# A two-block model on one core: modulation products shared with POOL, own PSUM banks in the mixers, and the context's norm in step with its loads

## The chip, the cores and the metric

The kernel runs on one core of a Trainium2 chip. A core has TensorE (matrix products, written PE in the profile, its weight loads PEld), VectorE (DVE), ScalarE (ACT), GpSimd (POOL) and SyncE (SP), which here issues most transfers. The metric is the device time of one execution in microseconds, in float32, from inputs in device memory to the output there; the median of several runs is given.

## The reference, cut to what matters

Two transformer-like models run one after the other on 256 tokens of width 1024. The first has two layers; the second has one layer with a context of 256 tokens of its own and ends in 32 experts.

```python
for l in range(2):                       # first block
    sh1, sc1, g1, sh2, sc2, g2 = split(silu(c) @ ada_w[l] + ada_b[l], 6)
    h = rmsnorm(x, norm_mix_w[l]) * (1 + sc1) + sh1
    x = x + g1 * mixer(h, ...)           # attention + mLSTM, gated, merged
    h = rmsnorm(x, norm_ffn_w[l]) * (1 + sc2) + sh2
    x = x + g2 * conv_ffn(h, ...)
x = rmsnorm(x, final_norm_w)
...                                      # second block
mod_c = silu(c_ctx) @ w_ada + b_ada      # modulation of the context
hc = rmsnorm(ctx, norm1) * (1 + sc1c) + sh1c
pc = hc @ w_in                           # keys, values, states of the context
...                                      # same for x; three mixers; experts
```

The modulation (the "adaptive" products) is a row vector of 1024 times a matrix of 1024 x 6144, four times in all: for both layers, for the context (a third of it) and for the second block.

## The kernel before

Activations lie transposed, as eight blocks of 128 channels by 256 tokens. A float32 product is made of three matmuls of a rounded high part and a low rest (`mm3`, `mm3n`, lines 474 to 476 and 487 to 489): weights come from memory in loads of 128 x 2048 floats (1 MB, `Stream.reach`, `load` at L442), each half of which ACT copies to `hi` (L451) and VectorE differences to `lo` (L453), three buffers of 1024 columns each. The buffers `raw` of the loads (three) are shared with the modulation matrices outside the context; in the context these have four of their own.

Modulation isn't done on TensorE. `ada` (L524 to L536) loads 128 x 2048 floats of the transposed matrix, and VectorE multiplies each half of 1024 with the broadcast row `c` and adds it up in one instruction (L533): 16 products for the context, 144 more in the background. A background generator is moved on by `tick()`, called after steps of the foreground, with a rate per tick; `ADA_PARTS` and `ADA_RATE` say which sixths of a modulation are made in which mixer or feed-forward, and how fast.

The order within each engine comes from a scheduler that plans with the program's order as priority; `in_order` ties the weight and modulation loads to the program's order on SP.

The stages: the context of the second block first (`context`, L1163), which needs the modulation of the context, the norm of `ctx` (`norm_mod`, `rstd_x`, `scaled`) and then projections from `h`: the first four column blocks at once (`proj4`: for each of eight blocks of `h` four column blocks in two banks of tag `d`), more from `proj`, `hgrn_ctx`, `na_norm`. Then rope tables, and for each of two layers a mixer (L660) and a feed-forward (L987). Beside the feed-forwards runs a recurrence on the context (`rwkv`), then comes the middle (three mixers of the second block), then the experts.

PSUM has eight banks, of tags d (2), a (3), y (2), f (1). In the mixer the latent projections use two d banks (`proj4`) and one y bank: `p2[:, :T]` for the last query block and `p2[:, T:]` for rope keys and gates (L707 to L709), then two d banks each for keys (`keys`), values (`pv`, L733) and queries.

Of the kernel before, what the change touches and what calls it, by code (L numbers as in the profile page):

```python
# [11 lines left out]
F32 = mybir.dt.float32  # L12
# [4 lines left out]
OP = mybir.AluOpType  # L17
AX = mybir.AxisListType
PSUM = bass.MemoryType.PSUM
P = 128  # L20
# [15 lines left out]
ADA_PARTS = (range(2, 6), range(6, 9), range(9, 14), range(14, 18))  # L36
ADA_RATE, RK_RATE, MID_RATES = (0.8, 0.45, 0.95, 0.6), 0.8, (0.6, 1.0, 1.0, 1.0, 0.6)
# [314 lines left out]
class Net:  # L352
# [153 lines left out]
    def proj4(self, st, h):  # L506

        ps = [self.ps("d") for _ in range(2)]
        for i, hk in enumerate(h):
            for c in range(4):  # L510
                self.mm3(ps[c // 2][:, c % 2 * T : c % 2 * T + T], st, [hk], i == 0 and c % 2 == 0, i == 7)
        return ps
# [10 lines left out]

    def ada(self, src, c, bias, mod, parts, pool=None):  # L524

        nc = self.nc
        for s in parts:
            for q in range(4 * s, 4 * s + 4):
                raw = self.load(src[q], pool, 3 if pool is None else CX_RAW)
                for r in range(2):  # L530
                    j = 2 * q + r
                    w = raw[:, r * 1024 : r * 1024 + 1024]
                    nc.vector.scalar_tensor_tensor(w, w, 0.5, c, OP.mult, OP.mult, accum_out=mod[:, j : j + 1])  # L533
                yield
            m = slice(8 * s, 8 * s + 8)
            nc.vector.tensor_tensor(mod[:, m], mod[:, m], bias[:, m], OP.add)  # L536
# [45 lines left out]
    def scaled(self, x, r, gain, shift):  # L582

        nc = self.nc
        hhi, hlo = self.pair(self.ap, 8, "h")
        for k in range(8):
# [5 lines left out]
            if k == 0:  # L592
                self.normed = a.ins
            b = nc.vector.scalar_tensor_tensor(hlo[:, k, :], t, shift[:, k : k + 1], hhi[:, k, :].bitcast(F32), OP.add, OP.subtract)  # L594
        self.normed_v = b.ins
        return self.parts((hhi, hlo), range(8))

    def norm_mod(self, x, norm, scale, shift, adds=True):

        gain = self.np.tile([P, 8], F32, tag="gain", name=self.uid("gain"))  # L600
        self.nc.vector.scalar_tensor_tensor(gain, scale, 1.0, norm, OP.add, OP.mult)
        return self.scaled(x, self.rstd_x(x, adds), gain, shift)
# [57 lines left out]
    def mixer(self, l, mp, x, mod):  # L660
# [4 lines left out]
        h = self.norm_mod(x, self.V("nmix" + s, 0, 8), mod[:, 8:16], mod[:, 0:8])  # L665
# [39 lines left out]
        p2 = self.ps("y")  # L705
        self.mm3(p2[:, :T], st, h)
        normed(ckv, 3, 2, 256)  # L707
        latent(2, p2[:, :T], self.V("qn" + s, 2))
        self.mm3(p2[:, T:], st, h)  # L709
# [15 lines left out]
        nc.vector.tensor_tensor(krm[64:128, :], p2[64:128, T:], self.cs[64:128, :], OP.mult)  # L725
        gi, gf = self.tmp(T, "gi", bufs=1, rows=8), self.tmp(T, "gf", bufs=1, rows=8)
        nc.vector.tensor_scalar(gi, p2[0:8, T:], self.V("gb" + s)[0:8], None, OP.add)
        nc.vector.tensor_scalar(gf, p2[32:40, T:], self.V("gb" + s)[32:40], None, OP.add)
# [4 lines left out]
        pv = [self.ps("d") for _ in range(2)]  # L733
# [214 lines left out]
        for j0 in (0, 4):  # L948
            pas, pbs = ([self.ps(t) for _ in range(2)] for t in "dy")
            for ps, yp in ((pas, yap), (pbs, ymp)):  # L950
                for q in range(4):
                    self.mm3(ps[q // 2][:, q % 2 * T : q % 2 * T + T], st, yp)
                    if q % 2 and ps is pbs:
# [7 lines left out]
                        self.tick()  # L961
# [120 lines left out]
    def first(self):  # L1082
        nc, x = self.nc, self.x
        with self.pool("cxm") as cxp, self.pool("cb") as self.cbp:
            with self.pool("rope") as rp:
# [5 lines left out]
                with self.phase("r", {}):  # L1091
                    self.rope_tables(rp)
# [70 lines left out]
    def context(self, cxp, rp):  # L1163
# [3 lines left out]
        with self.pool("cx") as cx, self.phase("c", {256: 6, 512: 5}):  # L1167
# [5 lines left out]
            for i, _ in enumerate(self.ada(A["ada2"], cc, self.V("adab2", 0, 48), self.mod_c, (0, 1), cx)):  # L1173
                if i == 1:
                    nc.sync.dma_start(self.vec, A["vecs"])
                    nc.sync.dma_start(xc, A["ctxT"].rearrange("p (k t) -> p k t", k=8))
                if i == 5:
                    st.reach()
            self.cb = self.silu_row(A["c_x"], nc.sync)
            h = self.norm_mod(xc, self.V("n1", 0, 8), self.mod_c[:, 8:16], self.mod_c[:, 0:8], False)  # L1180
# [7 lines left out]
            first = self.proj4(st, h)  # L1188
# [6 lines left out]
            self.hgrn_ctx(cx, h, st)  # L1195
            for _ in self.na_norm(st, h, self.V("nk"), [self.naK[:, i : i + 2, :] for i in (0, 2)], False, "a"):
                self.tick()
# [971 lines left out]
```

## Time and profile before

| | us |
|---|---|
| median of 3 runs | 1775.16 (1772.66 to 1775.33) |
| the profiled execution | 1772.79 |
| its span, first to last instruction | 1770.9 |
| TensorE busy | 1579.1 (89%) |
| VectorE busy | 1128.0 (64%) |
| ScalarE busy | 758.6 (43%) |
| POOL busy | 77.9 (4%) |

The mean granted clock of TensorE is 0.946 of full speed. The profile comes from one execution; "idle before" in a row is the time in which the engine did nothing ahead of that instruction, and the name behind it is what came last of what it waited for. Matmuls are pipelined: each has a duration longer than its distance from the next. Shares over the whole span mix stages of different kinds, so the rows below are taken from single stretches.

### The profile page before, as it was taken

The numbers are of one execution on the slowest core, as the hardware profiler recorded it, in microseconds if no ns is written. First come the engines' busy times: TensorE is split into PE (matmuls) and PEld (weight loads), VectorE is DVE, ScalarE is ACT, GpSimd is POOL, SyncE is SP. The second block draws the span as 40 slices with busy tenths as digits, with TensorE's granted clock in tenths as the row PEclk, the third lists the DMA queues.
The fourth block names the chain that finished last, engine by engine and source line by source line (L and its number), as shares of the span: only waits on it lengthen the run. The fifth ranks groups of instructions, "written<-read, shape, count | busy, mean of one in ns | idle before, by whom it ended". The sixth has DMA issues, their size and how long they took to land.

```text
span 1770.9 us, 32054 instructions
## 1 busy us (share of the span) xinstructions
PE 1579.1 (89%) x13278; PEld 1269.7 (72%) x13278; DVE 1128.0 (64%) x2167; ACT 758.6 (43%) x1256; POOL 77.9 (4%) x81
## 2 busy tenths in 40 slices
PE   3989999999998999989999999999989877776766
PEld 2988999899998899979999999878874312221211
DVE  7979878798887898879989778766662111011011
ACT  3566545664455654556454576464431100000000
POOL 0000000020010000001010101000000000000000
PEclk7999999999999999999999999998989889888888
DMA  9745675556674478565667543123369999999998
GB/s 392 312 142 191 242 281 204 209 207 221 217 250 143 169 266 319 216 237 179 239 228 289 194 171 114 67 98 134 144 249 403 419 417 416 417 416 419 419 417 340
DMA packets 76808, 460.78 MB, mean 260 GB/s; under 512 B 8563, under 2 KB 11123, under 8 KB 28147
## 3 DMA queue, kind: packets, MB, share of 16 engines
q1 hardware_dynamic: 74352, 452.45, 67.0%
q10 hardware_dynamic: 2306, 6.24, 1.0%
q8 instruction: 106, 1.74, 0.4%
q14 instruction: 44, 0.35, 0.1%
HBM read 457.61 MB, written 1.05 MB: 259 GB/s over the span
## 4 chain that ended last, share of the span: by engine, by line
PE 63%; DMA 23%; DVE 8%; ACT 4%; issue 2%; POOL 0%; SPq 0%; DVEq 0%; ACTq 0%; POOLq 0%
DMA ew<-in_wgu 11%; PE d L474 10%; PE d L476 10%; PE d L475 10%; DMA ew<-in_wdown 8%; PE y L474 4%; PE y L476 3%; PE y L475 3%; PE a L1392 3%; DVE lo L453 2%; PE d L2052 2%; DVE raw L533 2%; PE a L1981 1%; PE a L628 1%; DMA raw<-in_ws 1%
## 5 line engine op out<-in xcount | busy, mean ns | idle before, releaser
L451 ACT CAST hi<-raw 128x1024 fp32r<-128x1024 f32 x309 | 322.4, 1048 | 303.2 <-PE d L475 186.2
L453 DVE TENSOR_TENSOR lo<-raw,hi 128x1024 fp32r<-128x1024 f32 x309 | 379.1, 1233 | 90.3 <-ACT hi L451 88.5
L474 PE MATMUL d<-hhi,hi 128*128 128x256 f32 x1320 | 387.9, 295 | 29.4 <-ACT hhi L591 23.7
L475 PE MATMUL d<-hlo,hi 128*128 128x256 f32 x1320 | 381.3, 289 | 3.2 <-DVE hlo L594 1.7
L476 PE MATMUL d<-hhi,lo 128*128 128x256 f32 x1320 | 380.2, 288 | 0.2 <-DVE lo L453 0.2
L474 PEld LDWEIGHTS d<-hhi,hi 128*128 128x128 f32 x1320 | 258.4, 196 | 38.3 <-ACT hhi L591 26.3
L475 PEld LDWEIGHTS d<-hlo,hi 128*128 128x128 f32 x1320 | 259.3, 196 | 6.6 <-DVE hlo L594 2.9
L476 PEld LDWEIGHTS d<-hhi,lo 128*128 128x128 f32 x1320 | 259.0, 196 | 1.4 <-DVE lo L453 0.4
L2052 PE MATMUL d<-ew,xe 128*32 128x512 f32 x984 | 165.3, 704 | 56.5 <-DMA ew<-in_wgu 56.0
L533 DVE SCALAR_TENSOR_TENSOR raw<-raw,cb 128x1024 f32<-128x1024 f32 x160 | 193.9, 1228 | 5.4 <-DMA raw<-in_ada 5.0
L2052 PEld LDWEIGHTS d<-ew,xe 128*32 128x32 f32 x984 | 26.1, 116 | 170.5 <-DMA ew<-in_wgu 145.7
L2057 DVE SCALAR_TENSOR_TENSOR moa<-moa,d 128x512 f32<-128x512 f32 x8 | 5.5, 687 | 178.4 <-ACT moa L2056 178.4
L474 PE MATMUL y<-hhi,hi 128*128 128x256 f32 x352 | 100.8, 286 | 4.6 <-ACT raw L685 3.9
L476 PE MATMUL y<-hhi,lo 128*128 128x256 f32 x352 | 100.0, 285 | 0.9 <-DVE lo L453 0.9
L475 PE MATMUL y<-hlo,hi 128*128 128x256 f32 x352 | 99.6, 283 | 0.0
L2070 PE MATMUL y<-ew,mht 128*32 128x512 f32 x472 | 74.4, 687 | 26.6 <-DMA ew<-in_wdown 22.4
L2088 DVE SCALAR_TENSOR_TENSOR x<-f,mod_l,x 128x256 f32<-128x256 f32 x32 | 14.0, 479 | 127.8 <-PE f L2084 127.8
L459 POOL TENSOR_TENSOR hidl<-fgel,hidh 128x256 fp32r<-128x256 f32 x44 | 54.2, 1233 | 838.4 <-ACT hidh L458 817.3
L2056 ACT ACTIVATE moa<-d 128x512 f32<-128x512 f32 x8 | 4.8, 597 | 184.7 <-PE d L2052 184.7
L474 PEld LDWEIGHTS y<-hhi,hi 128*128 128x128 f32 x352 | 67.4, 192 | 6.1 <-ACT raw L685 4.7
L2070 PEld LDWEIGHTS y<-ew,mht 128*32 128x32 f32 x472 | 13.0, 117 | 78.3 <-DMA ew<-in_wdown 58.6
L476 PEld LDWEIGHTS y<-hhi,lo 128*128 128x128 f32 x352 | 67.4, 192 | 1.4 <-DVE lo L453 1.1
(676 smaller groups left out, 3193.7 us busy)
## 6 DMA issues: line engine op xcount, KB each, us to landing
raw<-in_ws SPq DMA_DIRECT2D x151, 1024.0 KB, 4.8
ew<-in_wgu SPq DMA_DIRECT2D x100, 1024.0 KB, 18.0
raw<-in_ada SPq DMA_DIRECT2D x80, 1024.0 KB, 4.9
ew<-in_wdown SPq DMA_DIRECT2D x46, 1024.0 KB, 19.7
ew<-in_wgu SPq DMA_DIRECT2D x46, 512.0 KB, 13.8
ew<-in_wdown SPq DMA_DIRECT2D x28, 512.0 KB, 12.5
two<-in_wgu SPq DMA_DIRECT2D x20, 256.0 KB, 8.4
two<-in_wdown SPq DMA_DIRECT2D x16, 256.0 KB, 8.1
```

Of the source, the lines that this page charges most:

```text
L451: f.append(nc.scalar.copy(hi_, raw))
L453: f.append(nc.vector.tensor_tensor(lo_, raw, hi_.bitcast(F32), OP.subtract))
L459: (eng or self.nc.vector).tensor_tensor(lo, src, hi.bitcast(F32), OP.subtract)
L474: nc.tensor.matmul(out, whi, hhi, start=first and i == 0, stop=False, **s)
L475: nc.tensor.matmul(out, whi, hlo, start=False, stop=False, **s)
L476: nc.tensor.matmul(out, wlo, hhi, start=False, stop=last and i == n - 1, **s)
L533: nc.vector.scalar_tensor_tensor(w, w, 0.5, c, OP.mult, OP.mult, accum_out=mod[:, j : j + 1])
L628: self.nc.tensor.transpose(out, in_, self.C("ident")[:k, :k])
L1392: nc.tensor.matmul(ps[r, g * 64 : g * 64 + 64], l_(g, p, r), r_(g, p, r), start=True, stop=True, skip_group_check=True)
L1981: nc.tensor.matmul(ps[:, k * P : k * P + P], xn[:, i, d : d + P], of(i), start=i == 0, stop=i == 1, skip_group_check=True)
L2052: nc.tensor.matmul(ps[32 * e : 32 * e + 32, :], xe[:, k, 32 * e : 32 * e + 32], w[e], start=k == 0, stop=k == 7, skip_group_check=True)
L2070: nc.tensor.matmul(py[q][32 * e : 32 * e + 32, :], ht[:, f * P + 32 * e : f * P + 32 * e + 32], w[e], start=f == 0, stop=f == 3, skip_grou ...
```

## The change

Four things are changed. (1) `ada_block`: of each modulation load outside the context's own, the first half is multiplied on POOL and summed by an ACT copy with accumulation, the second half stays on VectorE; in the context's own eight loads the first halves of four go that way. (2) In the context the modulation loads are taken in pairs (scale, shift), the bias added, two of eight blocks of `ctx` normed and scaled, and two steps of the first projection (`proj4_steps`) made after each pair; the norm of x for mixer 0 (`r0`) and the rope tables are put into the context. (3) In the mixer the second half of `p2` becomes a bank `pg` of tag y, and the values use y instead of d. (4) The sixths are dealt out as 4, 4, 4, 4 instead of 4, 3, 5, 4 with other rates, and the branch projections have no `tick()`.

```diff
--- before.py
+++ after.py
@@ -33,8 +33,8 @@
-ADA_PARTS = (range(2, 6), range(6, 9), range(9, 14), range(14, 18))
-ADA_RATE, RK_RATE, MID_RATES = (0.8, 0.45, 0.95, 0.6), 0.8, (0.6, 1.0, 1.0, 1.0, 0.6)
+ADA_PARTS = (range(2, 6), range(6, 10), range(10, 14), range(14, 18))
+ADA_RATE, RK_RATE, MID_RATES = (0.8, 0.45, 0.8, 0.45), 0.8, (0.6, 1.0, 1.0, 1.0, 0.6)
@@ -505,10 +505,21 @@
+        steps = self.proj4_steps(st, h)
+        while True:
+            try:
+                next(steps)
+            except StopIteration as e:
+                return e.value
+
+    def proj4_steps(self, st, h):
+
         ps = [self.ps("d") for _ in range(2)]
...
                 self.mm3(ps[c // 2][:, c % 2 * T : c % 2 * T + T], st, [hk], i == 0 and c % 2 == 0, i == 7)
+            if i < 7:
+                yield
         return ps
@@ -521,6 +532,15 @@
+    def ada_block(self, w, c, out, shared):
+
+        nc = self.nc
+        if shared:
+            nc.gpsimd.tensor_tensor(w, w, c, OP.mult)
+            nc.scalar.activation(w, w, AF.Copy, scale=0.5, accum_out=out)
+        else:
+            nc.vector.scalar_tensor_tensor(w, w, 0.5, c, OP.mult, OP.mult, accum_out=out)
+
     def ada(self, src, c, bias, mod, parts, pool=None):
@@ -528,9 +548,7 @@
                 for r in range(2):
-                    j = 2 * q + r
-                    w = raw[:, r * 1024 : r * 1024 + 1024]
-                    nc.vector.scalar_tensor_tensor(w, w, 0.5, c, OP.mult, OP.mult, accum_out=mod[:, j : j + 1])
+                    self.ada_block(raw[:, r * 1024 : r * 1024 + 1024], c, mod[:, 2 * q + r : 2 * q + r + 1], r == 0)
                 yield
@@ -581,25 +599,28 @@
-        nc = self.nc
-        hhi, hlo = self.pair(self.ap, 8, "h")
-        for k in range(8):
+        h = self.pair(self.ap, 8, "h")
+        self.scale_blocks(h, range(8), x, r, gain, shift)
+        return self.parts(h, range(8))
+
+    def scale_blocks(self, h, ks, x, r, gain, shift):
+        nc, (hhi, hlo) = self.nc, h
+        for k in ks:
             if k % 2 == 0:
...
             a = nc.scalar.activation(hhi[:, k, :], t, AF.Identity, bias=shift[:, k : k + 1])
-            if k == 0:
+            if k in (0, ks[0]):
                 self.normed = a.ins
...
         self.normed_v = b.ins
-        return self.parts((hhi, hlo), range(8))
-
-    def norm_mod(self, x, norm, scale, shift, adds=True):
+
+    def norm_mod(self, x, norm, scale, shift, r=None):
...
         self.nc.vector.scalar_tensor_tensor(gain, scale, 1.0, norm, OP.add, OP.mult)
-        return self.scaled(x, self.rstd_x(x, adds), gain, shift)
+        return self.scaled(x, self.rstd_x(x) if r is None else r, gain, shift)
@@ -662,7 +683,7 @@
         v2 = lambda ap: ap.rearrange("p (a t) -> p a t", a=2)
-        h = self.norm_mod(x, self.V("nmix" + s, 0, 8), mod[:, 8:16], mod[:, 0:8])
+        h = self.norm_mod(x, self.V("nmix" + s, 0, 8), mod[:, 8:16], mod[:, 0:8], self.r0 if l == 0 else None)
         self.tick()
@@ -702,11 +723,11 @@
             latent(q, p01[:, q * T : q * T + T], self.V("qn" + s, q))
-        p2 = self.ps("y")
-        self.mm3(p2[:, :T], st, h)
+        p2, pg = (self.ps("y")[:, :T] for _ in range(2))
+        self.mm3(p2, st, h)
         normed(ckv, 3, 2, 256)
-        latent(2, p2[:, :T], self.V("qn" + s, 2))
-        self.mm3(p2[:, T:], st, h)
+        latent(2, p2, self.V("qn" + s, 2))
+        self.mm3(pg, st, h)
@@ -722,15 +743,15 @@
         krm = mt([T], "krm")
-        nc.vector.tensor_tensor(krm[64:128, :], p2[64:128, T:], self.cs[64:128, :], OP.mult)
+        nc.vector.tensor_tensor(krm[64:128, :], pg[64:128], self.cs[64:128, :], OP.mult)
         gi, gf = self.tmp(T, "gi", bufs=1, rows=8), self.tmp(T, "gf", bufs=1, rows=8)
-        nc.vector.tensor_scalar(gi, p2[0:8, T:], self.V("gb" + s)[0:8], None, OP.add)
-        nc.vector.tensor_scalar(gf, p2[32:40, T:], self.V("gb" + s)[32:40], None, OP.add)
+        nc.vector.tensor_scalar(gi, pg[0:8], self.V("gb" + s)[0:8], None, OP.add)
+        nc.vector.tensor_scalar(gf, pg[32:40], self.V("gb" + s)[32:40], None, OP.add)
         keys(1)
...
         nc.scalar.copy(kf[64:128], bcn(pk[64:128, :T], 8))
-        pv = [self.ps("d") for _ in range(2)]
+        pv = [self.ps("y") for _ in range(2)]
         self.mm3n(pv, st, ckvp, 512, False)
@@ -958,7 +979,6 @@
                         self.split(m[0][:, j : j + 2, :], m[1][:, j : j + 2, :], v2(ta))
-                        self.tick()
         gh = self.np.tile([P, 8], F32, tag="gh", name=self.uid("gh"))
@@ -1088,8 +1108,6 @@
                 self.part = 1
-                with self.phase("r", {}):
-                    self.rope_tables(rp)
                 for l in range(2):
@@ -1170,14 +1188,31 @@
             st = Stream(self, "cx")
-            for i, _ in enumerate(self.ada(A["ada2"], cc, self.V("adab2", 0, 48), self.mod_c, (0, 1), cx)):
-                if i == 1:
-                    nc.sync.dma_start(self.vec, A["vecs"])
+            hp = self.pair(self.ap, 8, "h")
+            h = self.parts(hp, range(8))
+            steps, gain, first = self.proj4_steps(st, h), cx.tile([P, 8], F32, name="cgain"), None
+            mod, norm, bias = self.mod_c, self.V("n1", 0, 8), self.V("adab2", 0, 48)
+
+            for q in range(4):
+                for o in (4 + q, q):
+                    raw = self.load(A["ada2"][o], cx, CX_RAW)
+                    if o == 4:
+                        nc.sync.dma_start(self.vec, A["vecs"])
+                    for i in range(2):
+                        self.ada_block(raw[:, i * 1024 : i * 1024 + 1024], cc, mod[:, 2 * o + i : 2 * o + i + 1], i == 0 and q < 2)
+                    nc.vector.tensor_tensor(mod[:, 2 * o : 2 * o + 2], mod[:, 2 * o : 2 * o + 2], bias[:, 2 * o : 2 * o + 2], OP.add)
+                if q == 0:
                     nc.sync.dma_start(xc, A["ctxT"].rearrange("p (k t) -> p k t", k=8))
-                if i == 5:
-                    st.reach()
+                    r = self.rstd_x(xc, False)
+                b = slice(2 * q, 2 * q + 2)
+                nc.vector.scalar_tensor_tensor(gain[:, b], mod[:, 8 + 2 * q : 10 + 2 * q], 1.0, norm[:, b], OP.add, OP.mult)
+                self.scale_blocks(hp, range(2 * q, 2 * q + 2), xc, r, gain, mod[:, 0:8])
+                for _ in range(2):
+                    try:
+                        next(steps)
+                    except StopIteration as e:
+                        first = e.value
             self.cb = self.silu_row(A["c_x"], nc.sync)
-            h = self.norm_mod(xc, self.V("n1", 0, 8), self.mod_c[:, 8:16], self.mod_c[:, 0:8], False)
             with self.tc.issue_after(self.normed):
@@ -1185,7 +1220,6 @@
             pad = [cx.tile([P, 2, T + 2], F32, name=f"cpad{i}") for i in range(3)]
-            first = self.proj4(st, h)
             for i in range(3):
@@ -1193,6 +1227,9 @@
             self.hgrn_ctx(cx, h, st)
+
+            self.r0 = self.rstd_x(self.x)
+            self.rope_tables(rp)
             for _ in self.na_norm(st, h, self.V("nk"), [self.naK[:, i : i + 2, :] for i in (0, 2)], False, "a"):
...
```

## Rows read from the trace of the kernel before

**Rows 1.** Waits of TensorE: for what, us in total, times, longest us
```profile
PE d L2052 <- DMA ew<-in_wgu: 56.0, 71, 1.6
PE y L474 <- ACT raw L685: 3.9, 2, 2.0
PE d L487 <- DVE kf L719: 3.3, 2, 1.7
```

**Rows 2.** Stretches: busy us of PE, PEld, DVE, ACT, POOL; clock, DMA share, GB/s
```profile
40.00:1020.00 980.00, 938.44 (x8248) 900.43 (x8247) 826.33 (x1466) 548.62 (x869) 56.19 (x49) 0.98 0.63 226
1340.00:1760.00 420.00, 319.90 (x1852) 100.99 (x1844) 53.51 (x123) 32.09 (x66) 0.00 (x0) 0.87 1.02 417
```

**Rows 3.** The same view, shorter stretches
```profile
20.00:40.00 20.00, 3.83 (x15) 3.02 (x15) 18.50 (x35) 7.36 (x12) 0.00 (x0) 0.59 1.02 421
36.00:44.00 8.00, 6.62 (x30) 6.33 (x31) 8.00 (x18) 4.77 (x9) 0.00 (x0) 0.50 1.01 416
...
160.00:180.00 20.00, 20.00 (x166) 19.07 (x165) 19.02 (x45) 14.32 (x31) 0.00 (x0) 1.00 0.54 195
...
960.00:980.00 20.00, 20.00 (x170) 20.00 (x170) 19.94 (x35) 11.97 (x21) 3.39 (x4) 1.00 0.82 292
```

**Rows 4.** Timeline at the start (start us, us, what, idle before and its releaser)
```profile
13.78 2.19 ACT L561 ACTIVATE two<-xc 128x512 f32<-128x512 f32 x4 [7.42 <-DMA xc<-in_ctxT]
...
29.57 1.22 DVE L533 SCALAR_TENSOR_TENSOR raw<-raw,cb 128x1024 f32<-128x1024 f32 x1
33.01 1.22 DVE L533 SCALAR_TENSOR_TENSOR raw<-raw,cb 128x1024 f32<-128x1024 f32 x1
...
35.82 0.80 PE L474 MATMUL d<-hhi,hi 128*128 128x256 f32 x2 [14.79 <-ACT hhi L591]
```

**Rows 5.** Timeline of TensorE, instructions that it stood before
```profile
54.08 0.39 PE L474 MATMUL d<-hhi,hi 128*128 128x256 f32 x1 [1.85 <-ACT cpad L1216]
...
115.87 0.79 PE L474 MATMUL d<-hhi,hi 128*128 128x256 f32 x2 [5.33 <-ACT hhi L591]
...
134.47 0.38 PE L474 MATMUL y<-hhi,hi 128*128 128x256 f32 x1 [1.92 <-ACT raw L685]
...
144.77 0.50 PE L487 MATMUL d<-hi,lat 128*128 128x512 f32 x1 [1.67 <-DVE kf L719]
...
296.00 0.39 PE L474 MATMUL d<-ya,hi 128*128 128x256 f32 x1 [1.21 <-ACT hi L451]
...
546.14 0.39 PE L475 MATMUL y<-hidl,hi 128*128 128x256 f32 x1 [1.03 <-POOL hidl L459]
```

**Rows 6.** Timeline at mixer 0, three engines: its entry, then its keys
```profile
109.52 1.02 PE L572 MATMUL f<-two,ones 128*128 128x256 f32 x4
...
112.56 0.47 ACT L548 ACTIVATE rstd<-f,eps 128x256 f32<-128x256 f32 x1
115.31 1.31 ACT L591 ACTIVATE hhi<-two,mod 128x256 fp32r<-128x256 f32 x3 [0.55 <-DVE two L590]
...
135.84 0.69 DVE L459 TENSOR_TENSOR lat<-raw,lat 128x512 fp32r<-128x512 f32 x1 [0.35 <-ACT lat L458]
```

**Rows 7.** Single lines: count, duration in ns (least/median/most), when, shapes
```profile
L533 DVE SCALAR_TENSOR_TENSOR raw<-raw,cb x160: 1185/1219/1762, 8.0 to 967.9; 128x1024 f32<-128x1024 f32 x160
...
L459 POOL TENSOR_TENSOR hidl<-fgel,hidh x44: 726/1298/1825, 360.5 to 1008.3; 128x256 fp32r<-128x256 f32 x44
...
L1728 POOL TENSOR_TENSOR two<-two,kon x8: 994/999/1108, 1183.3 to 1283.4; 128x384 f32<-128x384 f32 x8
...
L451 ACT CAST hi<-raw x309: 1027/1047/1111, 26.2 to 1292.1; 128x1024 fp32r<-128x1024 f32 x155
...
L855 ACT ACTIVATION_READ_ACCUMULATOR esm<-a,mx x32: 192/197/206, 160.3 to 666.0; 128x1 f32 x32
```

**Rows 8.** Timeline of VectorE and POOL where both work
```profile
364.51 2.90 DVE L453 TENSOR_TENSOR lo<-raw,hi 128x1024 fp32r<-128x1024 f32 x2
...
364.71 1.61 POOL L459 TENSOR_TENSOR hidl<-fgel,hidh 128x256 fp32r<-128x256 f32 x1 [2.68 <-ACT hidh L458]
```

## The prediction

> **What bounds the kernel now.** I read the waits by engine first, then busy time by stretch, then the timelines of the stretches that the diff touches, and last the durations by line. TensorE's waits [rows 1] have three sizes. The largest name the expert weights: from 1340 to 1760 us the DMA share is 1.02 at 417 GB/s [rows 2], so the expert stage is bound by transfers, and the change touches nothing in it; what is saved ahead of it is saved at the end. The next is the first `hhi`, 14.79 us in the row of 35.82 [rows 4]: the start of the kernel. Then come small ones, `y` L474 behind ACT `raw` L685 and `d` L487 behind DVE `kf` L719, twice each, once per mixer.
>
> Between 40 and 1020 us TensorE is busy 938 of 980 us at a mean clock of 0.98 [rows 2]: the two mixers and feed-forwards are bound by TensorE, with some 42 us of gaps. VectorE is second: 826 of 980 us (84%), ACT 549. VectorE is near its limit only in places: 10 of the 49 stretches of 20 us there have it at 19.0 us or more (first and last in [rows 3]). So there are three things to gain: the start, the gaps with a name, and little else; and one to lose, VectorE's slack.
>
> **The start.** Now eight 1 MB loads of context modulation all come before the norm; VectorE's last product begins at 33.01, the first projection at 35.82 [rows 4], and TensorE is through its 96 matmuls at 52.2, where its next wait of 1.85 us begins [rows 5]. The transfers set this: 20 to 40 us has 421 GB/s; and TensorE has the lower of its two clock levels (0.50, 1.2 of 2.4 GHz) from 36 to 44 us, after it stood [rows 3]. After the change a pair of loads (scale, shift) frees two of eight blocks, and a quarter of the 96 matmuls follows each pair. The context `xc` is there at 13.78 [rows 4], behind the same five transfers as before; behind it now come six more modulation loads and two weight loads: 8 x 1.05 MB / 421 GB/s = 19.9 us, so the last pair lands at 33.7. Two products at 1.15 us a step (29.57 to 33.01 is three steps), bias, one scaling and the ACT copy, 3.6 us in all (with one product less, 33.01 to 35.82 took 2.8; the gain is ready earlier now), put the last pair's first matmul at 37.3. Its 24 matmuls at the low clock's 0.213 us (their spacing until 44 us) take 5.1: 42.4. VectorE must in that time also do 12 products, 4 or 5 splits and 16 scalings (some 28 us of work between 8 and 36 us), and it runs in order, so I add 1.6: the projection ends at 44 instead of 52, a gain of **8 us**. Bounds: 12 (no queueing on VectorE, clock up early) and -2 (VectorE held behind splits whose weights come late, as its two splits stood ahead of the last products before). What follows it doesn't starve: weights are used at one load (1 MB) per 5.8 us of matmul (48 at 0.12), and at 421 GB/s 2.4 MB come in that time.
>
> **Entry of mixer 0.** TensorE stands 5.33 us at 115.87 because the four sums for x's norm ran last, at 109.52, and `rstd` came at 112.56 behind a table load [rows 5, 6]. With r0 computed inside the context the norm waits only for the `h` buffer, which the context's last projection reads. The first block then costs an ACT copy (1.31 us for three at 115.31, [rows 6]) and a like VectorE difference, with hand-over about 1.2 us: 4.1 saved. The 15 matmuls at 0.213 instead of 0.12 after the stop cost 1.4, of which I count half: **4.8 us**. Bounds 0 (the modulation of x comes late) and 5.5. The rope tables are moved too: one transfer on SP, 15 small VectorE operations and two on ACT with a table load; they ran beside matmuls before that stop and will again: nothing (some 5 us if VectorE has no gap there).
>
> **Own PSUM banks, per mixer.** The key/gate projection waits 1.92 us for the reader of the other half of its bank [rows 5]. With its own bank it ends 1.9 us sooner, but the keys need the low half of the normed latent, written from 135.84 to 136.5 [rows 6], against 137.44 when they start now: 0.9 is gained. The value projection waits 1.67 us for the keys' banks; in `y` it finds both free (both have been read while the keys ran): 1.4, as the queries behind it may be a little late. (0.9 + 1.4) x 2 mixers = **4.6 us**; bounds 1.8 (the queries wait instead) and 7.2 (all four waits).
>
> **Fewer ticks, other parts.** Without ticks in the branch projections no modulation load lies between their weights. In that stretch TensorE waits 1.21 us for a cast [rows 5], whose weights arrived late behind buffers that modulation products still held, with 0.45 and 0.17 right after by the same timeline, and 1.83 in the second mixer. The loads move to the output projection, which has the same three buffers: I take **2 us** of 3.7; bounds 0 and 4.4. Moving four loads from mixer 1 to the first feed-forward and the rates move work between stages that are alike: counted with the next part.
>
> **Shared products.** 76 of 160 products leave VectorE, each 1.2 us with its accumulator read: 91 us. Each becomes a POOL product of 128x1024 and an ACT copy with accumulation. POOL has no such shape in this trace: 0.73 us at 256 columns and 0.99 at 384, undisturbed [rows 7], is 2.09 ns a column, so 2.33 us (estimate). ACT pays 1.05 for a copy of that width and 0.20 for the read: 95 us in all. It is free for 431 of the 980 us; but it runs in order, and a copy that waits for POOL holds the casts behind it.
>
> The price is on VectorE. At 364.51 two splits take 2.90 us instead of 2.44, and the POOL product at 364.71, worth 0.73, takes 1.61 [rows 8]: it waited for the first split and the second waited for it. POOL's `hidl` shows it in general, 1.30 us in the middle against 0.73 at least. So a POOL product of 2.33 us may hold VectorE for 0 (VectorE idle, or working from PSUM) to 2.33 us (next operation has two SBUF inputs, as splits and products have). Those are about two thirds of VectorE's work in a mixer, so I take 1.7: 76 x 1.7 = 129, less the 91 freed, is 38 us more of VectorE, on 154 us of slack between 40 and 1020. It reaches TensorE where VectorE is full, a fifth of the stretches: **8 us lost**. Bounds: a gain of 5 (TensorE's waits for late `cacc`, `est` and `qf`, four per mixer of 0.5 to 0.8 us, go) and a loss of 38. In the feed-forwards `hidl` can stand behind such a product; the wait of 1.03 us at the end of each [rows 5] may double, within that 8.
>
> The Trainium skill, "SBUF — State Buffer", section "Who interferes with whom", says that a VectorE instruction with two SBUF inputs and a GpSimd instruction that reads SBUF exclude each other for their whole length, while one with at most one SBUF input isn't touched. Rows 8 agree in both directions, and by that rule alone, with every product held against, the loss on VectorE would be 86 us and not 38; that is the first rival.
>
> **Sum.** 8 + 4.8 + 4.6 + 2 - 8 = 11.4 us. The profiled execution took 1772.8 us (span 1770.9); the median of the runs is 2.4 higher, at 1775.2. 1772.8 - 11.4 = 1761.4; between the two bases I say **1762**.
>
> **Rivals.**
> 1. *The products cost VectorE more than they free* (slower). Place: mixers and feed-forwards. All 76 hold it 2.33 us: 177 - 91 = 86 us, and half reaches TensorE: 43 against gains of 19.4, so 1772.8 + 23.6 = 1796. For it: rows 8, and VectorE at 84%. Against: a third of its work isn't held, and casts run ahead by three buffers of 2.9 us. It decides from 0.26 us of TensorE time per product. ACT waiting in order for POOL adds to it.
> 2. *The start or the entry doesn't arrive.* Eight megabytes must come in any case, VectorE works through 28 us of work in 28, and if the norm's blocks only trickle, the start gives 1 and the entry 2: 1772.8 - (3 + 4.6 + 2 - 8) = 1771.2, no change. That the change doesn't do what it says is this case: the order of issue is worked out from a plan, and x's squares ran early before without their sums doing so.
> 3. *VectorE is truly relieved.* POOL runs mostly in VectorE's gaps, and the waits for late VectorE results go: 8 + 4.8 + 4.6 + 2 + 5 = 24.4, so 1748. For it: the branch stalls. Against: rows 8.
>
> **Chances.** Forecast (1754 to 1769) 0.5, rival 1 0.17, rival 2 0.16, rival 3 0.17. The range of 1745 to 1781 takes in rivals 2 and 3 and the near end of rival 1, where half of its loss comes. Faster means below 1771.6, slower above 1778.7 (0.2% of 1775.2, what a measurement can tell): forecast, rival 3 and half of rival 2 are faster, 0.75; the other half and a little of rival 1 no change, 0.11; the rest slower, 0.14.
>
> **What would show it.** After: first projection in quarters from about 15 us, the last ending near 44; the entry's wait for `hhi` near 1 us; no wait of `y` L474 on `raw` and none of `d` L487 on `kf`; POOL products near 2.3 us alone and up to 3.5 when disturbed; splits with a mean above 1.23 us; VectorE's total between 40 and 1020 us up, not down. The prediction is wrong if the splits keep their 1.22 us beside POOL (rival 3), if the casts wait for ACT copies behind POOL by more than a quarter of a microsecond each (rival 1), or if the projection ends after 50 us (rival 2).

## The result, and the profile after

The changed kernel takes 1856.7 us (1855.5 to 1862.4) against 1774.1 (1772.7 to 1775.3): slower, ratio 1.0472, 95% interval 1.0448 to 1.0496. The profile after has a span of 1855.2 us.

| | before | after |
|---|---|---|
| TensorE busy | 1579.1 | 1604.1 |
| VectorE busy | 1128.0 | 1163.2 |
| ScalarE busy | 758.6 | 834.1 |
| POOL busy | 77.9 | 286.2 |
| first `hhi` of mixer 0 starts | 115.3 | 132.4 |
| last `hhi` of the second feed-forward starts | 803.0 | 867.8 |
| `xn`, the experts' input, starts | 1315.1 | 1399.2 |
| from there to the end | 455.8 | 456.0 |

The experts are as before; all 84 us are lost ahead of them, 17 before mixer 0 and the rest spread over mixers, feed-forwards and middle. First the waits of TensorE, which answer to [rows 1]:

```profile
PE d L2089 <- DMA ew<-in_wgu: 54.7, 67, 2.5
...
PE d L474 <- ACT hi L451: 15.6, 5, 4.7
PE d L476 <- DVE lo L453: 12.1, 11, 3.6
```

The two named bank waits of before are gone, and waits for cast (`hi`) and split (`lo`) of weights have come. Then the stretches of [rows 2], the first made longer to cover the same stages:

```profile
40.00:1100.00 1060.00, 955.11 (x8154) 911.81 (x8155) 863.27 (x1329) 616.57 (x1005) 254.31 (x120) 0.95 0.58 209
1424.00:1844.00 420.00, 320.27 (x1852) 100.49 (x1848) 53.49 (x123) 32.16 (x66) 0.00 (x0) 0.86 1.02 417
```

VectorE is not fuller (81% against 84%), and TensorE has a lower share of busy time and a lower clock: no other engine has become the bound. The durations, to [rows 7] (least/median/most ns):

```profile
L539 POOL TENSOR_TENSOR raw<-raw,cb x76: 2330/2544/3482, 12.7 to 1085.2; 128x1024 f32<-128x1024 f32 x76
...
L453 DVE TENSOR_TENSOR lo<-raw,hi x309: 1181/1219/3418, 23.0 to 1378.4; 128x1024 fp32r<-128x1024 f32 x155
```

The least product is the 2.33 us that was estimated; a split can now take 3.42 us, and the mean of all 309 is 1.34 us (1.23 before), as the prediction said a hold would show. And the timeline of VectorE and POOL, to [rows 8]:

```profile
49.40 2.99 DVE L616 SCALAR_TENSOR_TENSOR hlo<-two,mod_c,hhi 128x256 fp32r<-128x256 f32 x2
...
52.30 3.39 DVE L542 SCALAR_TENSOR_TENSOR raw<-raw,cb 128x1024 f32<-128x1024 f32 x1
...
55.63 2.90 DVE L1259 TENSOR_TENSOR mk<-cpad 128x256 f32<-128x256 f32 x2
...
49.56 8.34 POOL L539 TENSOR_TENSOR raw<-raw,cb 128x1024 f32<-128x1024 f32 x3 [25.86 <-DVE cb L532]
```

Three products of GpSimd run in a row, and each time one VectorE operation of 0.4 to 1.2 us takes some 2 us more. TensorE, to [rows 5], stands for the results:

```profile
48.54 0.73 PE L474 MATMUL d<-hhi,hi 128*128 128x256 f32 x2 [2.68 <-ACT hhi L613]
...
57.81 0.38 PE L474 MATMUL d<-hhi,hi 128*128 128x256 f32 x1 [2.66 <-ACT hi L451]
61.93 0.58 PE L476 MATMUL d<-hhi,lo 128*128 128x256 f32 x1 [3.62 <-DVE lo L453]
...
132.99 0.86 PE L474 MATMUL d<-hhi,hi 128*128 128x256 f32 x2 [0.48 <-ACT hhi L613]
```

The first projection, in quarters now, begins its last at 48.54 and TensorE is through at 55.15 (57.81 less its wait), later than 52.2 before and past the 50 us that the prediction named as a sign of rival 2. The entry's wait is 0.48, as forecast.

### The profile page after: what moved, and what is told of

Same layout as the page of the kernel before. It is cut to its first block, busy times and chain, and to the rows that moved or that the text cites. A ratio compares the mean times of both kernels' runs of the same rounds, so it can differ in the third digit from the quotient of the medians.

```text
span 1855.2 us, 32315 instructions
## 1 busy us (share of the span) xinstructions
PE 1604.1 (86%) x13278; PEld 1290.5 (70%) x13278; DVE 1163.2 (63%) x2030; ACT 834.1 (45%) x1405; POOL 286.2 (15%) x157
## 5 line engine op out<-in xcount | busy, mean ns | idle before, releaser
L453 DVE TENSOR_TENSOR lo<-raw,hi 128x1024 fp32r<-128x1024 f32 x309 | 413.2, 1343 | 105.6 <-ACT hi L451 103.8
L476 PE MATMUL d<-hhi,lo 128*128 128x256 f32 x1320 | 385.3, 292 | 9.4 <-DVE lo L453 9.3
L475 PE MATMUL d<-hlo,hi 128*128 128x256 f32 x1320 | 386.1, 293 | 6.8 <-DVE hlo L616 5.4
L539 POOL TENSOR_TENSOR raw<-raw,cb 128x1024 f32<-128x1024 f32 x76 | 212.1, 2792 | 636.8 <-DMA raw<-in_ada 336.9
L474 PEld LDWEIGHTS d<-hhi,hi 128*128 128x128 f32 x1320 | 262.7, 200 | 32.6 <-ACT hhi L613 11.5
L476 PEld LDWEIGHTS d<-hhi,lo 128*128 128x128 f32 x1320 | 263.5, 200 | 12.5 <-DVE lo L453 11.5
L475 PEld LDWEIGHTS d<-hlo,hi 128*128 128x128 f32 x1320 | 263.7, 200 | 10.4 <-DVE hlo L616 6.3
L542 DVE SCALAR_TENSOR_TENSOR raw<-raw,cb 128x1024 f32<-128x1024 f32 x84 | 139.6, 1666 | 29.0 <-DMA raw<-in_ada 28.9
L540 ACT ACTIVATE raw<-raw 128x1024 f32<-128x1024 f32 x76 | 80.5, 1060 | 148.4 <-POOL raw L539 148.2
## 6 DMA issues: line engine op xcount, KB each, us to landing
ew<-in_wdown SPq DMA_DIRECT2D x28, 512.0 KB, 12.6
```

The costliest lines, as they stand in the source:

```text
L453: f.append(nc.vector.tensor_tensor(lo_, raw, hi_.bitcast(F32), OP.subtract))
L474: nc.tensor.matmul(out, whi, hhi, start=first and i == 0, stop=False, **s)
L475: nc.tensor.matmul(out, whi, hlo, start=False, stop=False, **s)
L476: nc.tensor.matmul(out, wlo, hhi, start=False, stop=last and i == n - 1, **s)
L539: nc.gpsimd.tensor_tensor(w, w, c, OP.mult)
L540: nc.scalar.activation(w, w, AF.Copy, scale=0.5, accum_out=out)
```

## The experiments

Each kernel is set beside the kernel before on its chip; ratios are to that. One stretch is compared in all of them: from the first `hhi` of mixer 0 to the last of the second feed-forward, the same matmuls each time (5572 to 5577 are recorded). Its table stands behind the experiments. Each stretch comes from one profiled execution, and that of the kernel without sharing was the fastest of its five (1756.4 us), that of the product behind ACT's copy the slowest of its four (1852.4): differences of a few us between stretches aren't to be read.

**No sharing.** The changed kernel with all 160 products on VectorE.

```diff
-        if shared:
+        if False:
```

> The changed kernel with all 160 products on VectorE again; everything else of the change stays. If sharing is the whole loss, the time falls below the kernel before, to 1755 to 1768 us (the start, the entry of mixer 0 and the banks then bring their gain). If the other parts cost time by themselves, above all the start with its modulation buffers held longer, it stays above 1785 us.

Measured: 1764.0 us (1756.4 to 1765.6), ratio 0.9942 (0.9921 to 0.9962). Sharing is the whole loss, 92.6 us by medians from two chips (94 by the ratios), and the rest of the change is a gain.

**Sharing alone.** The kernel before, with the first half of each of the 72 background loads given to POOL and ACT.

```diff
-  nc.vector.scalar_tensor_tensor(w, w, 0.5, c, OP.mult, OP.mult, accum_out=...)
+  if r == 0:
+      nc.gpsimd.tensor_tensor(w, w, c, OP.mult)
+      nc.scalar.activation(w, w, AF.Copy, scale=0.5, accum_out=...)
+  else:
+      nc.vector.scalar_tensor_tensor(w, w, 0.5, c, OP.mult, OP.mult, accum_out=...)
```

> The kernel before with only the first half of each of the 72 background modulation loads on POOL and ACT. If sharing is the loss: 1835 to 1870 us. If the loss comes from what the parts do together (the pairs at the start and the hold of their buffers), only 1785 to 1800 us.

Measured: 1864.8 us (1861.8 to 1867.1), ratio 1.0509 (1.0486 to 1.0531). The same loss without the rest of the change.

**No product on POOL.** Only ACT's copy with its sum is left of the shared half.

```diff
-            nc.gpsimd.tensor_tensor(w, w, c, OP.mult)
             nc.scalar.activation(w, w, AF.Copy, scale=0.5, accum_out=out)
```

> The changed kernel without the POOL products: ACT copies and sums the loaded half as it is, so the modulation is left out by half and nothing waits for POOL. VectorE and ACT have the work of the changed kernel. If POOL is the cause, whether by holding VectorE or by making ACT wait, 1745 to 1765 us. If the ACT copies themselves (95 us) are too much for ACT, above 1800 us.

Measured: 1763.6 us (1760.7 to 1764.0), ratio 0.9929 (0.9907 to 0.995). VectorE is busy 1049.7 us against 1127.2 without sharing, ACT 834.1 against 756.7, and the kernel is only 0.5 us shorter. The two engines' parts in that aren't separated.

**Product last.** ACT copies first, so nothing but the load's buffer waits for POOL.

```diff
-            nc.gpsimd.tensor_tensor(w, w, c, OP.mult)
             nc.scalar.activation(w, w, AF.Copy, scale=0.5, accum_out=out)
+            nc.gpsimd.tensor_tensor(w, w, c, OP.mult)
```

> The changed kernel with the two instructions swapped: ACT copies and sums first, the POOL product comes after it and nobody but the load buffer waits for it; half of the modulation is left out so. POOL reads as much as before. If VectorE held by POOL is the loss: 1830 to 1860 us, splits still with a mean near 1.34 us. If ACT waiting in order for POOL is the loss: 1760 to 1785 us although the splits keep their 1.34 us.

Measured: 1846.5 us (1842.2 to 1852.4), ratio 1.0393 (1.0368 to 1.0418). So 10 us of the loss go with the swap (14 by the ratios), and 83 remain. The swap doesn't take out ACT's wait alone: ACT no longer waits 100.5 us for products in the stretch, but stands 51.0 us for modulation loads, whose buffers POOL now gives back last; VectorE stands 34.5 us for them. Without a POOL product the two wait 12.6 and 10.4 us for loads.

**Fills in place of products.** POOL as long at work, but it writes and reads nothing; ACT still waits behind it.

```diff
-            nc.gpsimd.tensor_tensor(w, w, c, OP.mult)
+            for _ in range(3):
+                nc.gpsimd.memset(w, 0.0)
```

> The changed kernel with each GpSimd product of a shared half load (2.8 us there, it reads the load and the gate row) replaced by three GpSimd fills of the same half load with zeros, which should take some 2 to 3 us together but read nothing; ScalarE's copy with its sum still waits behind them, and VectorE still does the other half. That half of the modulation is left out of the result. Theory 'GpSimd's reading stops VectorE': the splits (L453) come back to about 1.23 us, VectorE's busy time to about 1050 us, and the kernel to 1760 to 1780 us, as without any GpSimd work (1763.6). Rival 'the load buffer is given back later, or ScalarE stands behind GpSimd': the time of the GpSimd stage is what counts and the kernel stays at 1835 to 1857. Rival 'any GpSimd access, writes too': the splits stay at 1.34 and more, and the kernel over 1820.

Its total (5707 us) says nothing: with half of the modulation at zero TensorE has 27278 matmuls instead of 13278, presumably since the experts get other tokens. Until then it is comparable, and this is the clearest pair. The stretch, for fills, then for the changed kernel (columns as in [rows 2]):

```profile
117.40:793.60 676.20, 650.25 (x5577) 623.84 (x5577) 524.65 (x913) 436.74 (x727) 163.29 (x171) 0.98 0.62 225
```

```profile
132.40:867.80 735.40, 667.96 (x5572) 637.41 (x5572) 589.99 (x905) 430.41 (x722) 163.79 (x73) 0.97 0.57 205
```

POOL is busy 163 us in both. A load's buffer is held as long (in the stretch from issue to the end of its last use 10.4 and 10.6 us in the mean, before 11.4). With fills VectorE takes 65 us less and the stretch 59 less; without any POOL product it was 672.6. So it is neither POOL's time nor the buffers: what costs is that GpSimd *reads*, and VectorE is held by it. Nor is it that a fill is short, as products cut into four cost more (below). The pair doesn't separate VectorE's hold from ACT's wait, which grows with it, from 29.5 us for the fills to 100.5 for the products:

```profile
ACT raw L541 <- POOL raw L540: 29.5, 26, 3.4
```

```profile
ACT raw L540 <- POOL raw L539: 100.5, 36, 6.6
```

**Short products.** Four of 256 columns each.

```diff
-            nc.gpsimd.tensor_tensor(w, w, c, OP.mult)
+            for i in range(0, 1024, 256):
+                nc.gpsimd.tensor_tensor(w[:, i : i + 256], ..., c[:, i : i + 256], OP.mult)
```

> The changed kernel with each GpSimd product cut into four of 256 columns, by the rows about 0.73 us each and 2.9 us together, so the total for which VectorE can be held is the same, but none holds it longer than some 0.7 us at a time. Theory 'a split of the chain waits singly behind one whole product, over 2 us': the longest split falls from 3.4 us to about 2, and most of the loss goes: 1775 to 1800. Rival 'the total of held time counts, however cut': VectorE's busy time stays at about 1165 us and the kernel at 1840 to 1865.

Measured: 1931.7 us (1928.2 to 1940.8), ratio 1.09 (1.0867 to 1.0933): a miss, far worse. A piece takes 1.11 us in the mean and not 0.73. Where both work, pieces and VectorE's operations take turns: here four pieces worth 2.9 us take 4.84, and the split beside them, worth 1.22, takes 1.75.

```profile
822.35 4.84 POOL L540 TENSOR_TENSOR raw<-raw,cb 128x256 f32<-128x256 f32 x4 [9.35 <-DMA raw<-in_ada]
```

```profile
822.28 1.23 DVE L543 SCALAR_TENSOR_TENSOR raw<-raw,cb 128x1024 f32<-128x1024 f32 x1 [3.85 <-DMA raw<-in_ada]
...
823.43 1.75 DVE L453 TENSOR_TENSOR lo<-raw,hi 128x1024 fp32r<-128x1024 f32 x1
```

VectorE is held less, but ACT waits 191 us in the stretch for products, against 100.

**Short products last.** The same behind ACT's copy.

> The four short products of 256 columns once more, but after ScalarE's copy, so that ScalarE waits for nothing of GpSimd (half of the modulation is left out, as where one whole product came last, 1846.5). The kernel with short products first was at 1932 while VectorE was held less (548.7 us busy in the stretch of the mixers and feed-forwards, against 590.0). Theory 'there ScalarE stood in its order behind a product stretched to 4 us': without that wait it falls under the whole product's 1846, to 1790 to 1840. Rival 'the many short exclusions delay VectorE's and TensorE's chain as much': 1850 to 1930.

Measured: 1882.4 us (1872.7 to 1886.9), ratio 1.0636 (1.0587 to 1.0685). Some 50 us go with ACT's wait, but what remains is within the rival's range and more than with whole products in that place. Its pieces spread over more time, and with them the last use of each load buffer; ACT and VectorE, both in order, stand longer for the next loads. Product last, then short products last (waits of the stretch: us, times, longest):

```profile
ACT raw L539 <- DMA raw<-in_ada: 51.0, 27, 3.8
...
DVE raw L542 <- DMA raw<-in_ada: 34.5, 22, 4.4
```

```profile
ACT raw L539 <- DMA raw<-in_ada: 99.4, 40, 7.7
...
DVE raw L543 <- DMA raw<-in_ada: 71.0, 32, 6.3
```

**Half of the loads shared.**

```diff
-  self.ada_block(..., r == 0)
+  self.ada_block(..., r == 0 and q % 2 == 0)
```

> The changed kernel with only every second background load shared (36 products less; the 4 of the context's start stay). If each product costs TensorE the same, the loss falls in proportion: 1764 + 40/76 of 92 = about 1812 us. If VectorE takes some of them for nothing and pays for those that are over its slack, as the prediction has it, fewer than half cost anything: 1770 to 1795.

Measured: 1797.9 us (1797.7 to 1802.1), ratio 1.0137 (1.0115 to 1.0159). Between the two: 53% of the products cost 37% of the loss (1.95 of 5.30 points over no sharing). The first ones are by no means free, though they cost less each than the later ones.

**Half the length.** One product of 512 columns behind ACT's copy; the rest of it is left out.

```diff
             nc.scalar.activation(w, w, AF.Copy, scale=0.5, accum_out=out)
+            nc.gpsimd.tensor_tensor(w[:, :512], w[:, :512], c[:, :512], OP.mult)
```

> As many GpSimd products as in the changed kernel, each of the first 512 columns of its half load alone, some 1.26 us by the rows, after ScalarE's copy; the rest of the product and half of the modulation are left out. Between no product (1763.6) and the whole one in the same place (1846.5). Theory 'held time costs TensorE in proportion': 1790 to 1810. Rival 'a hold costs only what it is longer than a lead of some 1.2 us': 1764 to 1780. Rival 'each product costs the same, however long': 1820 to 1846.

Measured: 1788.7 us (1788.5 to 1794.0), ratio 1.0108 (1.0063 to 1.0153). VectorE is held 44.4 us (1094.1 less 1049.7) against 122.1 with whole products there, 36%; the loss is 1.79 points of 4.64, 39%. In proportion to the held time, and a hold is not free up to some length (the median itself is 1 us below that theory's range).

**One input.** POOL multiplies the half load by 1.0, ahead of ACT's copy; then the same behind it.

```diff
-            nc.gpsimd.tensor_tensor(w, w, c, OP.mult)
+            nc.gpsimd.tensor_scalar(w, w, 1.0, None, OP.mult)
```

> The changed kernel with each GpSimd product of two inputs replaced by a GpSimd multiplication of the same half load by the constant 1.0, which reads one input and writes it in place; ScalarE's copy waits behind it. The gate row is left out of that half of the modulation. By the fills, which read nothing (676.2 us for the stretch from mixer 0's norm to the last feed-forward's norm, against 672.6 without GpSimd work and 735.4 with the products). If any reading by GpSimd stops VectorE: a stretch over 700 us and the kernel over 1800. If only reading two inputs does: a stretch of 673 to 685 and the kernel at 1762 to 1775.

> The one-input GpSimd multiplication again, after ScalarE's copy, so that ScalarE waits for none of it (the gate row is left out of half of the modulation). Before the copy it took 1851.7 with VectorE held only 22 us in the stretch of the mixers and feed-forwards. If ScalarE's wait in its order was the cause there: 1765 to 1790. If what GpSimd's reading does to VectorE and to the loads is the cause: 1820 to 1850.

Measured: 1851.7 us (1849.2 to 1863.7), ratio 1.0475 (1.0423 to 1.0527); behind the copy 1813.9 (1810.4 to 1814.6), ratio 1.0208 (1.0165 to 1.0251). One input is enough to stop VectorE. But the hold is shorter:

```profile
403.05 3.10 POOL L539 TENSOR_SCALAR raw<-raw 128x1024 f32<-128x1024 f32 x1 [2.65 <-DMA raw<-in_ada]
...
403.43 1.26 DVE L1043 TENSOR_TENSOR fgel<-fgel,facc 128x256 f32<-128x256 f32 x1
404.62 0.41 DVE L1411 TENSOR_TENSOR NT<-a,kon 128x256 f32<-128x256 f32 x1
...
404.95 1.21 DVE L453 TENSOR_TENSOR lo<-raw,hi 128x1024 fp32r<-128x1024 f32 x1
```

An operation worth 0.42 takes 1.26, and then a split runs at its usual 1.21 while POOL is still at work. This isn't the place alone: in the two kernels no split takes more than 2.07 us, against 3.42 beside products. With so little held (22 us in the stretch), about half of the loss goes when ACT no longer waits; the kernel behind the copy lies between its two expectations. The other half, some 50 us, is far more than its VectorE hold (18 us in the stretch). Late loads go with it (waits in the stretch, to be set beside 12.6 and 10.4 us without a POOL product):

```profile
ACT raw L539 <- DMA raw<-in_ada: 78.6, 36, 5.4
```

```profile
DVE raw L542 <- DMA raw<-in_ada: 48.4, 30, 6.2
```

Whether they are the cause stays open: no run has a fourth load buffer, which would show it.

**More work for VectorE.** No POOL product; ahead of 76 products one more pass of VectorE over the same half.

```diff
+            nc.vector.scalar_tensor_tensor(w, w, 0.0, w, OP.mult, OP.add)
         nc.vector.scalar_tensor_tensor(w, w, 0.5, c, OP.mult, OP.mult, accum_out=out)
```

> The changed kernel with no GpSimd product; all 160 products on VectorE and, ahead of 76 of them, one more pass of VectorE over the same half load (w*0+w, 1.23 us by the rows), so VectorE has some 93 us more work than without sharing (1764.0), about as much as GpSimd's products held it for in the changed kernel, but in VectorE's own order. Theory 'a hold is dear because it stands in the order like work that nobody placed': VectorE's work there costs as little as taking 93 us of it away gained (0.5 us): 1764 to 1785. Rival 'any microsecond more on VectorE is paid at 0.7, hold or work': 1820 to 1850, and the price of a hold is no more than VectorE's load.

Measured: 1804.3 us (1799.1 to 1804.8), ratio 1.015 (1.0106 to 1.0195): between both theories. VectorE has 84.3 us more (1211.5 against 1127.2), the kernel 2.08 points, 37 us: 0.44 a microsecond. The pass also holds each load's buffer longer (13.5 us from issue to the end of its last use, against 11.1 without sharing), which is in that price.

**Banks alone, and all but the banks.** The kernel before with the mixers' own banks; then the one without sharing, with the old banks.

```diff
-        p2 = self.ps("y")
+        p2, pg = (self.ps("y")[:, :T] for _ in range(2))
...
-        pv = [self.ps("d") for _ in range(2)]
+        pv = [self.ps("y") for _ in range(2)]
```

> The kernel before with the mixers' own PSUM banks alone (the last latent, the gates' columns and the values' products each in a bank of its own, values under the name 'y'). By the prediction's term -4.6 us (bounds -1.8 and -7.2): 1768 to 1773. If the waits that go only move to the next instruction: 1774 to 1776.

> The changed kernel with no sharing (all 160 products on VectorE) and the mixers' old PSUM banks: what is left is the context's start in step, the norm and the rotary tables put earlier, the parts and rates, and one tick less. If the start and the entry of mixer 0 carry the gain of the kernel without sharing (1764 against 1776), this one is at 1765 to 1769, as the banks alone gave 3 us. If the banks carry it, it is at 1771 to 1776.

Measured: banks alone 1771.4 us (1763.2 to 1775.8), ratio 0.9975 (0.9957 to 0.9993), so 1 to 8 us; all but the banks 1764.9 (1756.0 to 1768.3), ratio 0.9956 (0.9933 to 0.9978), so 4 to 12 us. Both keep a gain; on its chip the kernel before is at 1768.4, so the expectation for the second, set on 1776, is to be read by its ratio: 7.8 us less, as if start, entry and parts carry most.

The stretch in the kernels that bear on the cause, from the same view (us):

| kernel | POOL busy | VectorE busy | TensorE busy, idle | stretch |
|---|---|---|---|---|
| before | 28 | 570 | 656, 32 | 687.7 |
| no sharing | 29 | 565 | 649, 26 | 674.6 |
| no product on POOL | 27 | 518 | 650, 23 | 672.6 |
| fills | 163 | 525 | 650, 26 | 676.2 |
| half the length | 110 | 546 | 658, 30 | 688.4 |
| half of the loads | 99 | 582 | 660, 39 | 699.2 |
| more work for VectorE | 31 | 622 | 664, 39 | 702.8 |
| one input, last | 173 | 536 | 661, 46 | 706.1 |
| product last | 160 | 592 | 667, 60 | 726.2 |
| one input | 182 | 540 | 675, 60 | 735.1 |
| changed | 164 | 590 | 668, 67 | 735.4 |
| short, last | 225 | 557 | 671, 74 | 745.1 |
| short | 238 | 549 | 687, 99 | 785.3 |

## Why the prediction was wrong

**The failed step** is in "Shared products": the net of 38 us more VectorE, which "reaches TensorE where VectorE is full, a fifth of the stretches: 8 us lost". The runs put 92.6 us in its place. VectorE's total without sharing, with no product on POOL, with the product behind ACT's copy, and after:

```profile
PE 1572.8 (90%) x13278; PEld 1266.9 (72%) x13278; DVE 1127.2 (64%) x2176; ACT 756.7 (43%) x1256; POOL 76.0 (4%) x81
```

```profile
PE 1585.3 (90%) x13278; PEld 1277.7 (73%) x13278; DVE 1049.7 (60%) x2034; ACT 834.1 (47%) x1401; POOL 77.4 (4%) x81
```

```profile
PE 1610.0 (87%) x13278; PEld 1293.9 (70%) x13278; DVE 1171.8 (63%) x2036; ACT 832.7 (45%) x1399; POOL 282.3 (15%) x157
```

```profile
PE 1604.1 (86%) x13278; PEld 1290.5 (70%) x13278; DVE 1163.2 (63%) x2030; ACT 834.1 (45%) x1405; POOL 286.2 (15%) x157
```

VectorE has 36.0 us more after the change, against 38 forecast. That is partly luck, as both parts of the net were too large by about as much: 77.5 us were freed and not 91, and 113.5 were held (1163.2 less 1049.7) and not 129, which is 1.49 us a product against 1.7. What failed is to net at all, since the parts don't have the same price, and to price the net by the slack:

- Freed work, with ACT's copies in its place, was worth nothing: 77.5 us less on VectorE and 77.4 more on ACT (no sharing to no product) gave 0.5 us. What it is worth without the copies no run shows.
- The product behind ACT's copy cost 83.0 us, with 122.1 us more on VectorE (no product to product last): 0.68 a microsecond. This isn't the price of the hold alone, since late loads come with it (85.5 us of waits of ACT and VectorE for them, against 23.0), and one input, with far less held, lost some 50 us in that place. How the 83 divide isn't shown.
- More work in VectorE's own order cost 0.44. So the theory that work in the planned order is nearly free fell too.
- The product ahead of ACT's copy, as in the changed kernel, cost 10.1 us more.

These three differences, -0.5 + 83.0 + 10.1 from one run to the next, make up the 92.6 lost to sharing: 1.2 us a product, where rival 1 was to decide from 0.26. Rival 1 was right in its sign and place, but it netted too (86 us, half of it to TensorE, 43). Its sign came as well: in the stretch ACT's copies wait 36 times for POOL, 2.8 us each in the mean, and the casts come behind them in ACT's order.

That 84% of VectorE left no room shows in TensorE's waits in the stretch: for VectorE 10.6 us without sharing and 38.9 after, for ACT 13.0 and 27.2. The reading, which no run shows by itself, is that the mean slack is many small gaps, while each weight goes in order through load, cast, split and matmul with three buffers; a hold of 2 us falls on one link, and everything behind it is later. Of the stretch's 60.8 us more, TensorE stands for 41.5. The other 19.3 are longer matmuls: the same ones take 648.7 us at a mean granted clock of 0.99 and 668.0 at 0.97, with more of the time at the lower of the two levels (1.2 and 2.4 GHz).

The rule of the Trainium skill that the prediction weighed ("SBUF — State Buffer", "Who interferes with whom") sets GpSimd instructions that read against those that only write; the fills (3.6 us in the stretch) and the products (62.8) agree. Its hold for the whole length fits the products, where a split takes up to 3.42 us, 2.2 more than alone. It doesn't fit the multiplication with one input, which takes 2.76 us at least: there no split takes more than 2.07 us, 0.85 more than alone.

**The start** (8 us forecast). Even without sharing it gave about 2.7: TensorE is through the projection at 49.5 (the next matmul's 51.14 less its wait), not at 44. The rows, to [rows 3 to 5], for the kernel without sharing:

```profile
20.00:40.00 20.00, 12.77 (x73) 11.46 (x72) 20.00 (x42) 7.83 (x12) 0.00 (x0) 0.83 1.01 419
```

```profile
43.18 0.80 PE L474 MATMUL d<-hhi,hi 128*128 128x256 f32 x2 [3.04 <-ACT hhi L613]
...
51.14 0.39 PE L474 MATMUL d<-hhi,hi 128*128 128x256 f32 x1 [1.62 <-ACT hi L451]
...
111.67 0.86 PE L474 MATMUL d<-hhi,hi 128*128 128x256 f32 x2 [0.48 <-ACT hhi L613]
137.51 0.51 PE L474 MATMUL d<-lat,hi 128*128 128x256 f32 x2 [0.20 <-ACT lat L458]
139.02 0.39 PE L475 MATMUL d<-lat,hi 128*128 128x256 f32 x1 [1.00 <-DVE lat L459]
```

VectorE is busy 20.00 of 20 us: the 1.6 us for its queueing seem to have been too few (no run tests this alone), and the last quarter begins at 43.18 and not at 37.3. After, the shared start is 5.4 us later still. POOL's first product begins at 12.74, though VectorE multiplied the other half of that load at 8.03; ACT stands in its order for it and comes late to the squares of the context (18.47, before 13.78):

```profile
12.74 2.33 POOL L539 TENSOR_TENSOR raw<-raw,cb 128x1024 f32<-128x1024 f32 x1 [12.30 <-issue]
...
15.10 1.06 ACT L540 ACTIVATE raw<-raw 128x1024 f32<-128x1024 f32 x1 [8.84 <-POOL raw L539]
...
18.47 1.66 ACT L579 ACTIVATE two<-xc 128x512 f32<-128x512 f32 x3
```

**The entry** (4.8). Its wait fell from 5.33 to 0.48 as forecast. But without sharing mixer 0's first matmul came only 4.2 us sooner (111.67, 115.87), less than start and entry by themselves: some of it was given back in the context, perhaps to the sums and rope tables that now stand there.

**Own banks** (4.6). Both waits went, and part of it returned where the prediction looked for it: keys wait 1.00 for the low half of the latent. And `d` L487 waits 3.0 us for `cacc` in the two mixers where it waited 1.6, in the kernel with the banks alone too. Alone the banks give 4.4 us (1.2 to 7.6).

**Ticks and parts** (2). The waits for casts and splits in the branch projections, 3.7 us in the two mixers before, are gone without sharing; one of 0.63 us has come in the output projection of mixer 0. All but the banks still shortens the stretch by 9.6 us (687.7 to 678.1), 5.4 of it in shorter matmuls, at a mean clock of 0.99 against 0.98, and 4.2 in waits. Which of ticks, parts and earlier sums does the rest wasn't taken apart, nor does one profile tell how much of the clock is chance.

Without sharing all terms came to 10 us (5.8 parts in 1000) where 19.4 were summed. So there the prediction was off by half in its sizes, not in its sign. The version that beats both kernels is that one, at 1764 us.

## What to carry to other kernels

Before work goes to GpSimd, ask whether it reads SBUF while VectorE has operations with two inputs there: the time is then taken from VectorE, at moments that its order didn't choose. Don't net freed against lost time on an engine that isn't the bound: here time freed at the price of copies on ACT was worth 0.006 us a microsecond, more work in order cost 0.44, and the products' hold, with the late loads that came with it, 0.68. A mean slack of 16% paid for little of it here, and shorter pieces, which took turns with VectorE's operations, made it worse in both places (1931.7 against 1856.7 us, and 1882.4 against 1846.5).

## What the hardware showed unexpectedly

- GpSimd's fills of 128x1024 (0.96 us each) leave splits at 1.23 us; a multiplication with one input, 2.76 us at least, is slower than the product of two inputs (2.33), but in the place shown lets VectorE go after 1.2 of its 3.1 us (by recorded spans, which are rough on POOL).
- GpSimd's first product began 4.7 us after VectorE had begun on the other half of the same load; fills in that place began at 7.78 us, so it is not the load. What it is wasn't looked for.
